# Down projection of a hybrid decoder block: which weight loads go to x1's old memory, and where one activation split stands

## The chip, the core and the metric

The kernel runs on one core of a Trainium2 chip. TensorE (PE) multiplies matrices, and PEld is its loading of weights; VectorE (DVE) and ScalarE (ACT) do elementwise work; GpSimd (POOL) does a little of it and issues some DMAs; SyncE (SP) issues most DMAs, in order. The metric is the time of one execution on the device, in microseconds (us).

## The reference, cut to what matters

One decoder block over 256 tokens of width 1024, all in float32: two token mixers (a gated linear recurrence and block attention), a gated merge, an output projection, a layer norm, a SwiGLU feed-forward network (FFN) of inner width 2816, and a second layer norm. The end is what matters here:

```python
x = layer_norm(DN_ALPHA * x + mixed, ln1_w, ln1_b)
h = jnp.einsum('bsd,df->bsf', x, w_ffn_in)
h_gate, h_up = jnp.split(h, 2, axis=-1)
y = jnp.einsum('bsf,fd->bsd', jax.nn.silu(h_gate) * h_up, w_ffn_down)   # the down projection
return layer_norm(DN_ALPHA * x + y, ln2_w, ln2_b)
```

## The kernel before

**Weights.** All weights come as 77 tiles of 128 x 2048 floats (1 MB), numbered 0 to 76 in the order of use. `stage` loads a tile into a buffer `raw` (SP), ScalarE rounds it to the high part `wh`, VectorE subtracts to get the low part `wl`, and TensorE makes three products of the high and low parts of weights and activations. The last reader of a raw buffer is VectorE's subtraction. The pools: `wraw` has three raw buffers, `whi` and `wlo` four each, taken in turn; `big` has 12 slots of the same size for everything else, and a slot is free when its last reader has run.

```python
wraw = pool("wraw", 3)
whi = pool("whi", 4)
wlo = pool("wlo", 4)
big = pool("big", 12)
```

**The down projection.** The FFN's inner width is worked in 11 blocks of two times 128 columns (`ffn_step`, with `q` the block's number), and block q's activations meet tile 66 and up of `w_ffn_down` in the order of `SEQUENCE`. `DOWN = "STTSTTSTPPP"` gives the kinds: the first eight tiles (66 to 73, blocks 2 to 9) are done with seven products instead of eight (`fast`), from a tile's four quarters and from sums of quarters; the last three (74 to 76, blocks 0, 1 and 10) are plain. A fast tile goes through `stage_fast` twice, as "corners" (three of its quarters, products `p1`, `p2`, `p3`) and as "sums" (four sums of quarters). For a tile of kind S (66, 69, 72) all four quarters are loaded with the corners and VectorE makes the sums in `cst` and a tile `sums` (lines 247 to 250). For a tile of kind T (67, 68, 70, 71, 73) DMAs made the sums in DRAM long before, and `rawsums` loads them.

**Where a raw load of a fast tile goes.** The sums of T tiles 68, 70, 71 and 73 go to a slot of `big`; the first T tile's sums (67) and all corners go to `wraw`. In `big` four slots come free about then: one half of x1's transposed parts `x1p` (the other half goes to `wb2`, the second norm's weights, loaded by GpSimd), `room` (the FFN's working memory), and the activations `as1`, `as2` of tiles that are done.

**The order.** In the last two FFN blocks and in the down projection TensorE, VectorE and ScalarE run in the order of the code (`manual_schedule`); SP's and GpSimd's order comes from a scheduler's own timeline. `fetch` runs ahead of TensorE by `LOOKAHEAD` = 3 tiles. The last block's `ffn_step` (block 10, plain) ends with `split(act_plain[q]...)`: ScalarE's cast `ap <- room` (line 191) and VectorE's subtraction (line 192).

**The end.** After tile 73's products `into_residual` (lines 1055 to 1064, VectorE) brings sums into `x1`; the plain tiles' products follow, the last ones in `edge` and `more`; VectorE, ScalarE and GpSimd make the second norm's statistics (lines 1104 to 1165) and SP stores four pieces.

Of the kernel before, what the change touches and what calls it, by code (L numbers as in the profile page):

```python
# [24 lines left out]
NF = FF // P  # L25
# [20 lines left out]
FAST = tuple(range(2, 2 + len(DOWN) - DOWN.count("P")))  # L46
PLAIN = tuple(q for q in range(NF // 2) if q not in FAST)
SEQUENCE = [PLAIN[DOWN[:i].count("P")] if s == "P" else FAST[i - DOWN[:i].count("P")] for i, s in enumerate(DOWN)]
SUMMED = [q for q, s in zip(SEQUENCE, DOWN) if s == "T"]
# [78 lines left out]
def hybrid_layer_kernel(ctx: ExitStack, tc, x, xw, vecs, bias, wts, ln1_w, ln1_b, ln2_w, ln2_b, consts, out):  # L128
# [12 lines left out]
    def slot(name, dt=F32):  # L141
        return big.tile([P, 2048], dt, tag="s8", name=name)

    def r32(ap):
        return ap.bitcast(F32)
# [32 lines left out]
    down = {t[1] // 2: i for i, t in enumerate(tiles) if t[0] == "w_ffn_down"}  # L178
# [6 lines left out]
    corners = {}  # L185
# [4 lines left out]
    def split(dst_h, dst_l, src):  # L190
        nc.scalar.copy(dst_h, src)
        nc.vector.tensor_sub(dst_l, src, r32(dst_h))
# [34 lines left out]
    quarters = lambda z: z.rearrange("p (b c) -> p b c", b=4)  # L227
# [13 lines left out]
    def stage_fast(i, kind):  # L241


        def make_sums(b):
            y, z = corners[i] = [v.rearrange("p (b c) -> p b c", b=2) for v in (
                cst, cp.tile([P, D], F32, tag="mv1", name=f"sums{i}"))]
            nc.vector.tensor_add(y, b[:, 1:3, :], b[:, 0:1, :].to_broadcast([P, 2, 512]))
            yield
            nc.vector.tensor_add(z[:, 0, :], b[:, 2, :], y[:, 0, :])
            nc.vector.tensor_add(z[:, 1, :], b[:, 3, :], z[:, 0, :])  # L250

        first = i == down[SUMMED[0]]
        raw = lambda: quarters(slot(f"raw{kind}{i}") if kind == "sums" and not first else
                               wraw.tile([P, 2048], F32, tag="raw", name=f"raw{kind}{i}"))
        h = quarters(whi.tile([P, 2048], F32R, tag="h", name=f"wh{kind}{i}"))
        l = quarters(wlo.tile([P, 2048], F32R, tag="l", name=f"wl{kind}{i}"))
        if kind == "corners":
            b = raw()
            n = 1 if i in summed else 0
            nc.sync.dma_start(b[:, n:4, :], quarters(wts[i])[:, n:4, :])  # L260
            sums = make_sums(b) if n == 0 else iter(())
            next(sums, None)
            h, l = h[:, 0:3, :], l[:, 0:3, :]
            nc.scalar.copy(h, b[:, 1:4, :])  # L264
            yield
            list(sums)
            nc.vector.tensor_sub(l, b[:, 1:4, :], r32(h))  # L267
            yield
        elif i in summed:
            z = raw()  # L270
            nc.sync.dma_start(z, quarters(summed[i]))
            nc.scalar.copy(h, z)  # L272
            yield
            nc.vector.tensor_sub(l, z, r32(h))  # L274
            yield
        else:
            for z, bs in zip(corners.pop(i), (slice(0, 2), slice(2, 4))):
                nc.scalar.copy(h[:, bs, :], z)
                yield
                nc.vector.tensor_sub(l[:, bs, :], z, r32(h[:, bs, :]))  # L280
                yield
        ready.append((h, l))

    def fetch(ahead=LOOKAHEAD):
        while state["next"] < len(loads) and len(ready) < 1 + ahead:
            list(stage())
        return ready.pop(0)
# [43 lines left out]
    def wide_pair(name, a, p, tag, twos=0):  # L331


        wh, wl = fetch()
        pss = []
        for f in range(2):
            ps = p.tile([P, 2, T], F32, tag=tag, name=f"{name}{f}")
            wcol = slice(f * P, (f + 1) * P)
            n = twos if f == 0 else 0
            for ks in [(k, k + 1) for k in range(0, 2 * n, 2)] + [(k,) for k in range(2 * n, KC)]:  # L340
                for k in ks:
                    nc.tensor.matmul(ps, wh[:, k, wcol], a.both(k), start=(k == 0), stop=False)  # L342
                for k in ks:
                    nc.tensor.matmul(ps[:, 0, :], wl[:, k, wcol], a[0, k, slice(0, T)],  # L344
                                     start=False, stop=(k == KC - 1))
            pss.append(ps)
        return pss
# [69 lines left out]
    with tc.manual_schedule(engines={ET.PE, ET.DVE, ET.Activation}):  # L417

        first = [slot(f"xw{k}")[:, 0:T + D] for k in range(KC)]
# [423 lines left out]
    def bcast(name, w, b):  # L843
        t = slot(name).rearrange("p (a d) -> p a d", a=2)
        nc.gpsimd.dma_start(t[:, 0, :], w[0].partition_broadcast(P))
        nc.gpsimd.dma_start(t[:, 1, :], b[0].partition_broadcast(P))
        return t
# [48 lines left out]
    act_plain = {q: apl[i // 2][:, i % 2] for i, q in enumerate(PLAIN)}  # L896

    def fast_parts(i):
        if i == 0:
            tiles = [klp.tile([P, H * P], F32R, tag="kl", name="ash"), cp.tile([P, D], F32R, tag="bgr", name="asl")]  # L900
        elif i == len(FAST) - 1:
            tiles = [apl[-1][:, 1].rearrange("p u k t -> p (u k t)"), cp.tile([P, 7 * P], F32R, tag="masks", name="asl7")]
        else:
            both = slot(f"as{i}", F32R)
            tiles = [both[:, 0:1024], both[:, 1024:2048]]
        return [z[:, 0:7 * P].rearrange("p (b t) -> p b t", b=7) for z in tiles]
# [94 lines left out]
    def ffn_step(j):  # L1001
        q = j // 2
        z = room[:, q % 2]
        gate, up = [z[:, b:b + 4, :].rearrange("p (f t) c -> p f (t c)", f=2) for b in (0, 4)]
        for nm, p, tag, s in [("g", mm, "mm", gate), ("u", aux, "aux", up)]:
            for f, ps in enumerate(wide_pair(f"f{nm}{j}", x1p, p, tag)):
                nc.scalar.copy(s[:, f, :], ps[:, 1, :])
                nc.vector.tensor_add(s[:, f, :], ps[:, 0, :], s[:, f, :])
            if nm == "g":
                nc.scalar.activation(s, s, AF.Silu)  # L1010
        nc.vector.tensor_mul(gate, gate, up)
        if q in PLAIN:
            split(act_plain[q][:, 0], act_plain[q][:, 1], gate)
            return

        nc.vector.tensor_sub(z[:, 4, :], z[:, 0, :], z[:, 2, :])
        nc.vector.tensor_sub(z[:, 5, :], z[:, 4, :], z[:, 1, :])
        nc.vector.tensor_sub(z[:, 6, :], z[:, 1, :], z[:, 0, :])
        nc.vector.tensor_add(z[:, 7, :], z[:, 3, :], z[:, 5, :])
        act_fast[q] = fast_parts(FAST.index(q))  # L1020
        split(*act_fast[q], z[:, 1:8, :])

    for j in range(EARLY, NF - 2 * ORDERED, 2):
        ffn_step(j)

    with tc.manual_schedule(engines={ET.PE, ET.DVE, ET.Activation}):
        for j in range(NF - 2 * ORDERED, NF, 2):
            ffn_step(j)
        wb2 = bcast("wb2", ln2_w, ln2_b)
        bank = lambda p, n: p.tile([P, 512], F32, tag="aux" if p is aux else "mm", name=n)  # L1030
        p2, p4, p1, p5 = [bank(mm, f"wp{i}") for i in (2, 4, 1, 5)]
# [9 lines left out]
        def fast(q):  # L1041
            ah, al = act_fast[q]
            for products in [((p1, 0, 0), (p2, 2, 2), (p3, 6, 1)),
                             ((p4, 1, 3), (p5, 3, 0), (p6, 4, 2), (p7, 5, 1))]:
                wh, wl = fetch()
                for ps, a, b in products:
                    stop = q == FAST[-1] and (ps in shared or ps is p2)
                    nc.tensor.matmul(ps, ah[:, a, :], wh[:, b, :], start=(q == begins[id(ps)]), stop=False)
                    nc.tensor.matmul(ps, ah[:, a, :], wl[:, b, :], start=False, stop=False)
                    nc.tensor.matmul(ps, al[:, a, :], wh[:, b, :], start=False, stop=stop)  # L1050
# [17 lines left out]
        for i, q in enumerate(SEQUENCE):  # L1068
            if q in FAST:
                fast(q)  # L1070
                if q == FAST[-1]:
                    into_residual()
                continue
            tile_q = [(2 * q,) + fetch()]
            if i < len(SEQUENCE) - HOLD_DOWN:
                for part in late:
                    rows_pass([part], lhs, 1, tile_q, first=2 * begins[id(part[0])], **ends)
            else:
                held += tile_q
            for part in early:  # L1080
                rows_pass([part], lhs, 0, tile_q, first=2 * begins[id(part[0])], **ends)
# [9 lines left out]
        sums = sm.tile([P, 2 * HOLD_DOWN], F32, tag="bst", name="wsum")  # L1091
# [113 lines left out]
```

## Time and profile before

| | |
|---|---|
| median of 3 runs | 488.55 us (488.53 to 488.66) |
| the profiled execution | 488.99 us, span 487.2 us |
| granted TensorE clock, mean | 0.998 |
| TensorE (PE), busy | 477.8 us, 98% |
| VectorE (DVE), busy | 387.9 us, 80% |
| ScalarE (ACT), busy | 293.8 us, 60% |
| GpSimd (POOL), busy | 57.6 us, 12% |
| DMA, all queues | 108.70 MB, mean 223 GB/s |

The profile has one page and views that are asked of the trace: windows (busy time of each engine in a stretch), timelines (start, duration, engine, line, operation, tiles; in brackets the engine's idle time before it and what ended it), the chain of waits followed back from the end, and the DMA view (issues, with the time until the data has landed). Times are us from the span's start. A matmul's shown duration overlaps the next one's: the distance of starts is what counts. `wp` is any of the products' PSUM banks.

### The profile page before, as it was taken

How to read it: one execution, taken by the hardware profiler on the slowest of the kernel's cores; microseconds unless marked ns; L12 is line 12 of the kernel's file. 1: busy time of each engine (PE TensorE's matmuls, PEld its weight loads, DVE VectorE, ACT ScalarE, POOL GpSimd, SP SyncE). 2: the span in 40 equal slices, each digit the busy share in tenths (PEclk: the TensorE clock that was granted, in tenths of full speed). 3: DMA queues.
4: the chain of work that ended last, by engine and by line, in shares of the span. 5: the costliest groups of instructions: out<-in, count | busy, mean ns of one | idle time of the engine just before them, and what ended most of it. 6: DMA issues, size and time to landing. Idle time of an engine off the chain costs nothing.

```text
span 487.2 us, 7433 instructions
## 1 busy us (share of the span) xinstructions
PE 477.8 (98%) x2956; PEld 408.8 (84%) x2956; DVE 387.9 (80%) x503; ACT 293.8 (60%) x407; POOL 57.6 (12%) x62
## 2 busy tenths in 40 slices
PE   8999999999999999999999999999999999999994
PEld 8888888788899888888888888888888888877884
DVE  4979895799947889998567778754887779689995
ACT  6698666447565787765743353455565564566762
POOL 0000000000024522422002001012110000000120
PEclk9999999999999999999999999999999999999999
DMA  8977438522853354468979853599999654299642
GB/s 307 414 308 262 174 120 297 214 105 88 295 200 112 118 206 166 160 219 279 264 270 283 227 221 139 187 295 291 301 243 300 204 199 154 92 414 381 220 111 87
DMA packets 21667, 108.70 MB, mean 223 GB/s; under 512 B 2432, under 2 KB 4224, under 8 KB 11904
## 3 DMA queue, kind: packets, MB, share of 16 engines
q1 hardware_dynamic: 16128, 98.13, 54.7%
q0 software_dynamic: 5360, 9.96, 10.4%
q8 instruction: 23, 0.38, 0.3%
q10 hardware_dynamic: 144, 0.13, 0.1%
q14 instruction: 12, 0.10, 0.1%
HBM read 105.59 MB, written 11.53 MB: 240 GB/s over the span
## 4 chain that ended last, share of the span: by engine, by line
PE 86%; DVE 6%; DMA 3%; issue 2%; ACT 1%; DVEq 0%; POOLq 0%; POOL 0%; SPq 0%; ACTq 0%
PE fu L342 7%; PE fg L342 7%; PE fg L344 3%; PE fu L344 3%; PE hq L342 3%; PE mq L342 2%; PE mk L342 2%; DMA rawsums<-sums 2%; PE mv L393 2%; PE gb L393 2%; PE hg L393 2%; PE hf L367 2%; PE hq L344 2%; PE mv L395 2%; PE ga L393 2%
## 5 line engine op out<-in xcount | busy, mean ns | idle before, releaser
L223 DVE TENSOR_TENSOR wl<-raw,wh 128x2048 fp32r<-128x2048 f32 (+1 forms) x70 | 160.4, 2296 | 55.4 <-ACT wh L221 55.1
L221 ACT CAST wh<-raw 128x2048 fp32r<-128x2048 f32 (+1 forms) x70 | 131.6, 1887 | 58.8 <-PE fg L342 14.0
L342 PE MATMUL fg<-x1p,wh 128*128 128x512 f32 x144 | 50.5, 394 | 0.0
L342 PE MATMUL fu<-x1p,wh 128*128 128x512 f32 x144 | 50.4, 394 | 0.0
L344 PE MATMUL fg<-x1p,wl 128*128 128x256 f32 x144 | 40.0, 278 | 0.0
L344 PE MATMUL fu<-x1p,wl 128*128 128x256 f32 x144 | 39.9, 277 | 0.0
L342 PEld LDWEIGHTS fu<-x1p,wh 128*128 128x128 f32 x144 | 27.0, 187 | 6.2
L342 PEld LDWEIGHTS fg<-x1p,wh 128*128 128x128 f32 x144 | 27.0, 187 | 6.1
L344 PEld LDWEIGHTS fg<-x1p,wl 128*128 128x128 f32 x144 | 27.1, 188 | 0.1
L344 PEld LDWEIGHTS fu<-x1p,wl 128*128 128x128 f32 x144 | 27.1, 188 | 0.0
L745 POOL TENSOR_TENSOR rtk<-rtk,cst 128x512 f32<-128x512 f32 x4 | 6.2, 1560 | 163.7 <-ACT rtk L743 163.7
L342 PE MATMUL hq<-xp,wh 128*128 128x512 f32 x64 | 22.2, 394 | 0.0
L344 PE MATMUL hq<-xp,wl 128*128 128x256 f32 x64 | 17.7, 277 | 0.0
L342 PE MATMUL mq<-xp,wh 128*128 128x512 f32 x48 | 17.0, 398 | 0.0
L342 PE MATMUL mk<-xp,wh 128*128 128x512 f32 x48 | 16.7, 395 | 0.0
L235 POOL DMA_DIRECT2D sums<-sums x10 | 8.1, 810 | 66.9 <-DMA sums<-in_wts_dram 33.6
L267 DVE TENSOR_TENSOR wlcorners<-rawcorners,whcorners 128x1536 fp32r<-128x1536 f32 x8 | 14.0, 1752 | 2.1 <-ACT whcorners L264 2.1
L342 PEld LDWEIGHTS hq<-xp,wh 128*128 128x128 f32 x64 | 12.0, 188 | 2.8
L235 POOL DMA_DIRECT2D sums<-in_wts_dram x10 | 8.4, 988 | 41.1 <-DMA sums<-in_wts_dram 41.1
L274 DVE TENSOR_TENSOR wlsums<-rawsums,whsums 128x2048 fp32r<-128x2048 f32 x5 | 11.4, 2287 | 2.2 <-ACT whsums L272 2.2
L344 PE MATMUL mq<-xp,wl 128*128 128x256 f32 x48 | 13.2, 281 | 0.0
L264 ACT CAST whcorners<-rawcorners 128x1536 fp32r<-128x1536 f32 x8 | 11.8, 1476 | 1.7 <-DMA rawcorners<-in_wts_dram 1.7
(371 smaller groups left out, 1339.7 us busy)
## 6 DMA issues: line engine op xcount, KB each, us to landing
raw<-in_wts_dram SPq DMA_DIRECT2D x68, 1024.0 KB, 4.9
sums<-in_wts_dram SPq DMA_DIRECT2D x10, 512.0 KB, 8.8
rawsums<-sums SPq DMA_DIRECT2D x5, 1024.0 KB, 9.1
xw<-in_xw_dram SPq DMA_DIRECT2D x6, 640.0 KB, 9.4
rawcorners<-in_wts_dram SPq DMA_DIRECT2D x5, 768.0 KB, 6.0
rawcorners<-in_wts_dram SPq DMA_DIRECT2D x3, 1024.0 KB, 8.1
sums<-in_wts_dram POOLq DMA_DIRECT2D x10, 256.0 KB, 9.1
sums<-sums POOLq DMA_DIRECT2D x10, 256.0 KB, 6.5
```

The costliest lines, as they stand in the source:

```text
L221: nc.scalar.copy(h[:, ks, :], raw[:, ks, :])
L223: eng.tensor_sub(l[:, ks, :], raw[:, ks, :], r32(h[:, ks, :]))
L235: more = lambda dst, src: nc.gpsimd.dma_start(dst, src, accum_op=ALU.add)
L264: nc.scalar.copy(h, b[:, 1:4, :])
L267: nc.vector.tensor_sub(l, b[:, 1:4, :], r32(h))
L274: nc.vector.tensor_sub(l, z, r32(h))
L342: nc.tensor.matmul(ps, wh[:, k, wcol], a.both(k), start=(k == 0), stop=False)
L344: nc.tensor.matmul(ps[:, 0, :], wl[:, k, wcol], a[0, k, slice(0, T)], start=False, stop=(k == KC - 1))
L367: nc.tensor.matmul(ps, wh[:, kk, wcol], xp.both(k), start=False, stop=False)
L393: nc.tensor.matmul(pss[t], ah[:, kk, ts], wh[:, k, :], start=(kk == 0), stop=False)
L395: nc.tensor.matmul(pss[t], ah[:, kk, ts], wl[:, k, :], start=False, stop=(kk == KC - 1))
L745: nc.gpsimd.tensor_mul(tmp, tmp, bc(sin))
```

## The change

Two things. In `stage_fast` the raw loads that go to `big` are now the corners, from the fourth fast tile on (69 to 73); all sums of T tiles, and the corners of 66, 67 and 68, go to `wraw`. In the last block the split of its activations is left to a later place: `ffn_step` returns `gate`, and the split is written behind `fast(FAST[0])`, the products of tile 66. In code that is after the fetches that `fast` made.

```diff
-        first = i == down[SUMMED[0]]
-        raw = lambda: quarters(slot(f"raw{kind}{i}") if kind == "sums" and not first else
+        beside = kind == "corners" and i not in [down[q] for q in SEQUENCE[0:3]]
+        raw = lambda: quarters(slot(f"raw{kind}{i}") if beside else
                                wraw.tile([P, 2048], F32, tag="raw", name=f"raw{kind}{i}"))
...
         if q in PLAIN:
-            split(act_plain[q][:, 0], act_plain[q][:, 1], gate)
-            return
+            if q < NF // 2 - 1:
+                split(act_plain[q][:, 0], act_plain[q][:, 1], gate)
+            return gate
...
-            ffn_step(j)
+            last_gate = ffn_step(j)
...
                 fast(q)
+                if q == FAST[0]:
+                    split(act_plain[PLAIN[-1]][:, 0], act_plain[PLAIN[-1]][:, 1], last_gate)
                 if q == FAST[-1]:
```

SP's loads from tile 68's corners on, before (the first number in a name is the tile's; the last is a buffer's):

```order
L260 DMA rawcorners68_3984<-in_wts_dram 128x1536
L271 DMA rawsums68_4002<-sums4_85 128x2048
L260 DMA rawcorners69_4017<-in_wts_dram 128x2048
L271 DMA rawsums70_4072<-sums6_86 128x2048
L260 DMA rawcorners70_4054<-in_wts_dram 128x1536
L260 DMA rawcorners71_4087<-in_wts_dram 128x1536
L271 DMA rawsums71_4105<-sums7_87 128x2048
L271 DMA rawsums73_4175<-sums9_88 128x2048
L260 DMA rawcorners72_4120<-in_wts_dram 128x2048
L260 DMA rawcorners73_4157<-in_wts_dram 128x1536
```

The same place on SP now:

```order
L260 DMA rawcorners68_3982<-in_wts_dram 128x1536
L260 DMA rawcorners69_4017<-in_wts_dram 128x2048
L271 DMA rawsums68_4002<-sums4_85 128x2048
L271 DMA rawsums70_4072<-sums6_86 128x2048
L271 DMA rawsums71_4105<-sums7_87 128x2048
L260 DMA rawcorners70_4054<-in_wts_dram 128x1536
L260 DMA rawcorners71_4087<-in_wts_dram 128x1536
L271 DMA rawsums73_4175<-sums9_88 128x2048
L260 DMA rawcorners72_4120<-in_wts_dram 128x2048
L260 DMA rawcorners73_4157<-in_wts_dram 128x1536
```

The corners of 69 moved ahead of the sums of 68, and the sums of 71 ahead of the corners of 70 and 71; raw74 to raw76 follow in both. What frees the memory of each now: 69 x1p's half (TensorE's last `fu` product), 70 `room` (the split of the last block's activations), 71 and 72 `as1` and `as2` (TensorE's products of tiles 67 and 68), 73 the corners of 69; the sums of 68 the corners of 67, those of 70 the sums of 67, those of 71 the corners of 68, those of 73 the sums of 68 (VectorE's subtractions).

ScalarE where the last block ends and the down projection begins, the difference:

```order
 L1007 COPY room_3056<-fu201_3932 128x256
+L272 CAST whsums67_3965<-rawsums67_3967 128x2048
+L264 CAST whcorners68_3980<-rawcorners68_3982 128x1536
 L191 CAST ap1_2624<-room_3056 128x512
-L272 CAST whsums67_3967<-rawsums67_3969 128x2048
-L264 CAST whcorners68_3982<-rawcorners68_3984 128x1536
 L272 CAST whsums68_4000<-rawsums68_4002 128x2048
 L264 CAST whcorners69_4015<-rawcorners69_4017 128x1536
```

The cast of the last block's activations moved behind two casts of weights, and nothing else moved here. VectorE's subtractions moved in the same way; TensorE's order is the same.

## The prediction

> In what follows c68 is the load of tile 68's corners (`rawcorners68`), s68 that of its sums (`rawsums68`), wlc68 and wls68 the VectorE subtractions that end their splits, and raw76 the last plain load.
>
> **What bounds the kernel now.** First the page's head.
>
> ```profile
> span 487.2 us, 7433 instructions
> PE 477.8 (98%) x2956; PEld 408.8 (84%) x2956; DVE 387.9 (80%) x503; ACT 293.8 (60%) x407; POOL 57.6 (12%) x62
> ```
>
> TensorE is busy for 98% of the span. The change touches the down projection alone, so I next read the windows there: length, busy time of PE, PEld, DVE, ACT and POOL with counts, granted clock, DMA share, GB/s.
>
> ```profile
> 430.00:440.00 10.00, 8.61 (x36) 6.47 (x36) 8.81 (x8) 6.61 (x5) 0.00 (x0) 1.00 1.02 424
> 440.00:450.00 10.00, 10.00 (x45) 7.97 (x44) 10.00 (x7) 6.86 (x5) 0.00 (x0) 1.00 0.95 366
> 450.00:460.00 10.00, 10.00 (x46) 8.22 (x45) 9.93 (x9) 8.15 (x6) 0.72 (x1) 1.00 0.56 199
> ```
>
> TensorE's only loss is in 430 to 440, where the DMA engines are full (share 1.02, 424 GB/s). From 440 to 460 VectorE is as full as TensorE: whatever delays VectorE before 440 is not made up. TensorE's timeline (start, duration) shows the stalls:
>
> ```profile
> 429.45 0.39 PE L1050 MATMUL wp<-whcorners,as 128*128 128x512 f32 x1
> 429.68 0.39 PE L1048 MATMUL wp<-whsums,as 128*128 128x512 f32 x1
> 430.19 0.50 PE L1049 MATMUL wp<-wlsums,as 128*128 128x512 f32 x1
> 430.53 0.39 PE L1050 MATMUL wp<-whsums,as 128*128 128x512 f32 x1
> ...
> 434.86 0.39 PE L1048 MATMUL wp<-whsums,as 128*128 128x512 f32 x1
> 435.27 0.50 PE L1049 MATMUL wp<-wlsums,as 128*128 128x512 f32 x1
> 435.61 0.40 PE L1050 MATMUL wp<-whsums,as 128*128 128x512 f32 x1
> ...
> 437.90 0.39 PE L1048 MATMUL wp<-whcorners,as 128*128 128x512 f32 x1
> 439.53 0.50 PE L1049 MATMUL wp<-wlcorners,as 128*128 128x512 f32 x1 [1.25 <-DVE wlcorners L267]
> 439.87 0.39 PE L1050 MATMUL wp<-whcorners,as 128*128 128x512 f32 x1
> ```
>
> Starts are 0.23 apart (429.45 to 429.68), so two steps take 0.46. The sums of tile 67 lose 0.85 - 0.46 = 0.39 us, those of 68 lose 0.29, the corners of 69 lose 1.51. The chain of waits (start, length, what) says behind what these lie:
>
> ```profile
> 423.04 7.84 DMA rawsums<-sums
> ...
> 430.98 1.92 ACT whsums L272
> ...
> 432.93 2.29 DVE wlsums L274
> 435.22 1.15 DVE cst L247
> ...
> 457.71 5.25 DMA raw<-in_wts_dram
> ...
> 465.01 2.29 DVE wl L223
> ```
>
> s68 lands at 430.88, ScalarE splits it, and from 432.93 on VectorE runs without a pause; at 457.71 raw76 is issued, and its VectorE work at 465.01 leads into the second layer norm. So two loads set this stage: s68 at its head, raw76 at its end. The change moves both.
>
> **Part 1: the split of `last_gate`.** It goes behind the casts of s67 and c68, on ScalarE and VectorE. ScalarE's rows, then VectorE's:
>
> ```profile
> 425.38 0.62 ACT L191 CAST ap<-room 128x512 fp32r<-128x512 f32 x1 [1.96 <-DVE room L1011]
> 425.91 1.91 ACT L272 CAST whsums<-rawsums 128x2048 fp32r<-128x2048 f32 x1
> ...
> 433.46 1.48 ACT L264 CAST whcorners<-rawcorners 128x1536 fp32r<-128x1536 f32 x1 [0.56 <-DMA rawcorners<-in_wts_dram]
> ...
> 438.79 1.48 ACT L264 CAST whcorners<-rawcorners 128x1536 fp32r<-128x1536 f32 x1
> ...
> 456.26 1.91 ACT L221 CAST wh<-raw 128x2048 fp32r<-128x2048 f32 x1
> ...
> 480.61 0.47 ACT L1110 ACTIVATE z<-more,n2sum 128x256 f32<-128x256 f32 x1 [0.39 <-PE more L861]
> ```
>
> ```profile
> 426.03 0.69 DVE L192 TENSOR_TENSOR ap<-room,ap 128x512 fp32r<-128x512 f32 x1 [0.69 <-ACT ap L191]
> ...
> 443.33 2.29 DVE L274 TENSOR_TENSOR wlsums<-rawsums,whsums 128x2048 fp32r<-128x2048 f32 x1
> ...
> 455.93 1.75 DVE L267 TENSOR_TENSOR wlcorners<-rawcorners,whcorners 128x1536 fp32r<-128x1536 f32 x1
> 457.60 2.28 DVE L274 TENSOR_TENSOR wlsums<-rawsums,whsums 128x2048 fp32r<-128x2048 f32 x1
> ...
> 467.22 0.68 DVE L1055 SCALAR_TENSOR_TENSOR x<-x,wp 128x512 f32<-128x512 f32 x1
> ...
> 478.46 0.22 DVE L1155 TENSOR_SCALAR n2sum<-wp,n2sum 128x1 f32<-128x1 f32 x1 [0.25 <-PE wp L861]
> ```
>
> ScalarE waited 1.96 us for VectorE and worked 0.53 before it came to s67. That goes: s67's cast starts 425.91 - 1.96 - 0.53 = 423.4, 2.5 earlier, and wls67 is 2.5 earlier too. Tile 67's stall of 0.39 goes. The moved split costs 0.62 and 0.69 on two engines that now wait for s68 until past 433: nothing. Its readers are tile 10's products, 30 us later: nothing.
>
> **Part 2: c69 ahead of s68.** On SP c69 takes s68's place and slot (x1's second half, free when the last `fu` product has read it), and s68 takes c69's (free after wlc67). Their rows on SP, and the DMA view of their two issues, with the time from issue to landing; last, s67, issued at 405 into an idle queue:
>
> ```profile
> 423.04 0.33 SPq L271 DMA_DIRECT2D rawsums<-sums  x1
> 423.98 0.33 SPq L260 DMA_DIRECT2D rawcorners<-in_wts_dram  x1
> ```
>
> ```profile
> rawsums<-sums SPq DMA_DIRECT2D x1, 1024.0 KB, 7.8
> ```
>
> ```profile
> rawcorners<-in_wts_dram SPq DMA_DIRECT2D x1, 1024.0 KB, 9.4
> ```
>
> ```profile
> rawsums<-sums SPq DMA_DIRECT2D x1, 1024.0 KB, 4.7
> ```
>
> The second landed at 423.98 + 9.4 = 433.4, 2.5 after the first; 1.05 MB at 424 GB/s are 2.47 us. So the two stood in line, and each took its share of a full queue. Both have the same size, and both issue times stay, so I take c69 to land at 430.88 and s68 at 433.36: **+2.48 us**. The lower bound is 0 (s68 lands as now, whatever is ahead of it), or even 4.7 after its issue, at 428.7; the upper is 2.48 and a little more. I take the end that the two landings show.
>
> Behind s68 on ScalarE and VectorE, in order, stand c69's cast, its sums and all later splits, although c69 is there already. wls68 starts at 433.36 + 0.10 + 1.92 + 0.03 = 435.41, not 432.93. TensorE, 0.39 ahead, comes to it at 434.7 and now stalls some 3.1 us, where it stalled 0.29. The 1.51 for the corners of 69 stay, since they are four VectorE instructions behind wls68. The rest is VectorE's unbroken row: all of it, and TensorE, +2.48.
>
> The Trainium skill ("DMA: Bandwidth & Descriptors", section "Queues, rings and completion order") says that each DMA engine takes descriptors in ring order, but that a later transfer may complete before an earlier one, so that completion is not first in, first out for an issuing engine. By that s68 could land no later than now, and the sum would be the second rival's below; the trace bears it out little, since the two landings kept their order by one whole transfer.
>
> **Part 3: the loads after these.** s71 goes ahead of c70 and c71. With s70 at 435.85 (one transfer behind s68), s71 lands near 438.3, c70, 0.75 MB, near 440.2; its cast stood at 438.79 and is now due at 441.27. It fits by 1.1 us. That is what is late next. raw74 waits for wls70 now: 443.33 + 2.29 + 2.48 = 448.1, some 10 us before its cast (456.26 + 2.48): nothing. c72 and c73 are ahead of their casts in the same way.
>
> **Part 4: raw76.** The pool `wraw` has three buffers, taken in turn. Before, the three loads ahead of raw76 in it were c73, raw74 and raw75, so it waited for the reader of c73, wlc73 (455.93 + 1.75 = 457.68). Now they are s73, raw74 and raw75, so it waits for wls73, the next VectorE instruction: 457.60 + 2.28 = 459.88. That is **+2.2 us** on top of the 2.48. Nothing covers it: the chain above goes through this load. With 5.0 to 5.25 us to landing (the chain's 5.25) raw76's subtraction comes 4.4 to 4.7 late, at 469.5 rather than 465.01.
>
> TensorE hardly minds. It took the product that needs it here:
>
> ```profile
> 469.27 0.39 PE L860 MATMUL wp<-wl,ap 128*128 128x512 f32 x1
> ```
>
> at 469.27 + 2.48 = 471.75, and the subtraction ends at 471.8 to 472.0: 0.0 to 0.3. But the residual (467.22 on) and the second norm stand behind it on VectorE in one row. Before the end this row has two rests, 0.25 us for TensorE's `edge` (478.46) and 0.39 on ScalarE for `more` (480.61), and these take up 0.64.
>
> **Sum.** 2.48 + 2.2 = 4.7 at raw76's wait, less up to 0.25 for a shorter landing, less 0.64: +3.8 to +4.1; I take +4.0. The profiled execution took 488.99 (span 487.2), 0.44 above the median of the runs, 488.55. It becomes 493.0, and the median 492.5.
>
> **Rivals.**
> - *TensorE sets the end, raw76's lateness is absorbed.* If the norm's VectorE row has more rest than the two I count, what is left is TensorE's shift: 2.48 + 0.0 to 0.3 = +2.7, 491.2. For it: TensorE's last product is waited for today. Against it: from 467.22 to 478.46 TensorE makes this VectorE row rest for 0.25 only.
> - *s68 lands as now.* Then part 2 costs nothing, c70 (440.2 against 438.79, mostly covered by VectorE's backlog) some 0.3, raw76 2.2, less 0.64: about +1.7, 490.2. Against it: the 2.48 between the two landings. The Trainium skill's rule above points here.
> - *Not slower: the queue holds nothing back.* If the 7.84 us of s68 were its own and not the line's, and it now came after 4.7 us like s67, it would land at 428.7; wls68 would start 2.2 earlier, which cancels raw76's 2.2, and the three stalls go: -0.6 to 0, 488.2. It decides from a landing of s68 before 429.5. Against it: a share of 1.02.
> - *Worse: c70 or c71 come late too.* If the line moves 1.1 us slower than I have it, each further us lands on VectorE: 493.6.
>
> **How the numbers follow.** The forecast has 0.70, then 0.10, 0.06, 0.07 and 0.07 for the rivals in order. The range runs from the second rival's 490.2 to 493.8, just above the last: 0.93 of the cases, less the forecast's own tails. This kernel's runs cannot tell less than 0.2%, 0.98 us, from no change; only the third rival is within or beyond it on the fast side: faster 0.03, same 0.04, slower 0.93.
>
> **What would show it.** In the trace after: TensorE's stall before the sums of 67 gone; c69 landed near 430.9 and s68 near 433.4, with ScalarE waiting for s68 about 6 us; a TensorE stall of some 3 us before wls68's products; VectorE without a pause from 435.4 to 464; raw76 issued near 462.4, and VectorE or ScalarE, not TensorE, released last. A landing of s68 at 431 or earlier, or an end released by `more`, would make me wrong.

## The result, and the profile after

The changed kernel takes 492.21 us (median of 6 runs, 491.9 to 494.12) against 488.54 us (488.33 to 488.82) of the kernel before beside it: a ratio of 1.0079, 95% interval [1.0063, 1.0095]: slower by 0.8%, clear of the noise. The profiled execution took 492.29 us, its span 490.5 us at a granted clock of 0.997.

The chain of waits after, at the same places as before (start, length, what):

```profile
423.85 9.26 DMA rawsums<-sums
...
433.20 1.92 ACT whsums L272
...
435.14 2.29 DVE wlsums L274
437.44 1.14 DVE cst L247
...
459.82 2.29 DVE wlsums L274
...
462.13 4.78 DMA raw<-in_wts_dram
...
468.96 2.29 DVE wl L223
471.25 0.59 DVE x L1056
```

s68 landed at 423.85 + 9.26 = 433.1 and not at 430.88, wls68 began at 435.14 and not at 432.93, and raw76 was issued at 462.13 instead of 457.71, right behind wls73 instead of wlc73. The same windows as before (length; PE, PEld, DVE, ACT and POOL busy; clock; DMA share; GB/s):

```profile
430.00:440.00 10.00, 7.48 (x32) 5.65 (x31) 4.79 (x5) 4.33 (x3) 0.00 (x0) 1.00 1.01 424
440.00:450.00 10.00, 8.77 (x38) 6.67 (x37) 10.00 (x8) 8.63 (x6) 0.00 (x0) 1.00 0.86 344
450.00:460.00 10.00, 10.00 (x45) 8.26 (x45) 9.93 (x9) 7.11 (x6) 0.00 (x0) 1.00 0.51 184
```

VectorE is busy for 4.79 us of the ten from 430 on, where it had 8.81, with the DMA engines as full as before (424 GB/s in both). The rows of ScalarE, VectorE and TensorE there, with idle time and its end in brackets:

```profile
423.18 1.92 ACT L272 CAST whsums<-rawsums 128x2048 fp32r<-128x2048 f32 x1
...
426.38 0.62 ACT L191 CAST ap<-room 128x512 fp32r<-128x512 f32 x1
433.20 1.91 ACT L272 CAST whsums<-rawsums 128x2048 fp32r<-128x2048 f32 x1 [6.20 <-DMA rawsums<-sums]
...
441.01 1.47 ACT L264 CAST whcorners<-rawcorners 128x1536 fp32r<-128x1536 f32 x1
```

```profile
425.14 2.29 DVE L274 TENSOR_TENSOR wlsums<-rawsums,whsums 128x2048 fp32r<-128x2048 f32 x1
...
435.14 2.29 DVE L274 TENSOR_TENSOR wlsums<-rawsums,whsums 128x2048 fp32r<-128x2048 f32 x1 [5.45 <-ACT whsums L272]
...
443.88 1.75 DVE L267 TENSOR_TENSOR wlcorners<-rawcorners,whcorners 128x1536 fp32r<-128x1536 f32 x1
```

```profile
429.32 0.39 PE L1051 MATMUL wp<-whcorners,as 128*128 128x512 f32 x1
429.54 0.39 PE L1049 MATMUL wp<-whsums,as 128*128 128x512 f32 x1
429.77 0.39 PE L1050 MATMUL wp<-wlsums,as 128*128 128x512 f32 x1
...
434.08 0.39 PE L1051 MATMUL wp<-whcorners,as 128*128 128x512 f32 x1
435.17 0.51 PE L1049 MATMUL wp<-whsums,as 128*128 128x512 f32 x1 [0.70 <-ACT whsums L272]
437.49 0.51 PE L1050 MATMUL wp<-wlsums,as 128*128 128x512 f32 x1 [1.82 <-DVE wlsums L274]
...
441.75 0.50 PE L1050 MATMUL wp<-wlcorners,as 128*128 128x512 f32 x1 [1.23 <-DVE wlcorners L267]
```

The cast of s67 runs at 423.18 instead of 425.91 and TensorE passes to the sums of 67 without a pause. What that wins, ScalarE and VectorE then spend waiting for s68.

### The profile page after: what moved, and what is told of

It is laid out like the page before. It is cut to its first block, busy times and chain, and to the rows that moved or that the text cites. A ratio compares the mean times of both kernels' runs of the same rounds, so it can differ in the third digit from the quotient of the medians.

```text
span 490.5 us, 7432 instructions
## 1 busy us (share of the span) xinstructions
PE 478.2 (97%) x2956; PEld 409.4 (83%) x2956; DVE 387.7 (79%) x503; ACT 293.5 (60%) x407; POOL 57.6 (12%) x62
## 4 chain that ended last, share of the span: by engine, by line
PE 82%; DVE 9%; DMA 3%; issue 2%; ACT 2%; DVEq 0%; POOLq 0%; POOL 0%; ACTq 0%
PE fg L342 6%; PE fu L342 5%; PE fg L344 3%; PE hq L342 3%; PE fu L344 3%; PE mq L342 2%; PE mk L342 2%; DMA rawsums<-sums 2%; DVE wlcorners L267 2%; PE mv L393 2%; PE gb L393 2%; PE hg L393 2%; PE hf L367 2%; PE hq L344 2%; PE ga L393 1%
## 5 line engine op out<-in xcount | busy, mean ns | idle before, releaser
L272 ACT CAST whsums<-rawsums 128x2048 fp32r<-128x2048 f32 x5 | 9.6, 1912 | 7.4 <-DMA rawsums<-sums 6.2
```

## The experiments

Theory: the split costs and brings nothing; s68 behind c69 in the line costs some 2.2 us, and raw76's wait for wls73 as much again, less a little slack at the end. The rivals: the moved split has a part in the loss; the lateness of raw76 is absorbed; s68's landing alone doesn't matter. Each run stands beside the kernel before on the same chip, which had a median of 488.9 us with the first four runs, 488.63 with the next four and 488.74 with the last two.

### 1. The split alone

The changed kernel, its raw loads in the places of before:

```diff
-        beside = kind == "corners" and i not in [down[q] for q in SEQUENCE[0:3]]
-        raw = lambda: quarters(slot(f"raw{kind}{i}") if beside else
+        first = i == down[SUMMED[0]]
+        raw = lambda: quarters(slot(f"raw{kind}{i}") if kind == "sums" and not first else
```

> Only the split of the last block's activations is moved; the raw loads keep their old places. Theory (the time lies in two loads, sums of 68 and raw76): 488.5, within 0.2% of before; tile 67's TensorE stall goes, and the one for the sums of 68 grows by the same 0.4 us. Rival (the split, now between casts of weights, costs): 490 or more. Rival (the split's move is worth its stall): 488.1.

488.57 us (11 runs), ratio 0.9993 [0.9984, 1.0001]: the same as before. VectorE's rows of wls67 and wls68:

```profile
424.56 2.29 DVE L274 TENSOR_TENSOR wlsums<-rawsums,whsums 128x2048 fp32r<-128x2048 f32 x1
...
432.02 2.29 DVE L274 TENSOR_TENSOR wlsums<-rawsums,whsums 128x2048 fp32r<-128x2048 f32 x1 [2.90 <-ACT whsums L272]
```

wls67 comes early, and VectorE then waits 2.90 us for s68's split where it waited 1.12. The later split also frees `room` later, so s70, which still goes there, is issued at 429.19 (426.79 before), behind c70 and c71, and lands at 440.46; ScalarE waits 1.21 us for it and VectorE not at all. An engine that is freed in front of a late load waits for it longer.

### 2. The places alone

The changed kernel with the split of `last_gate` back in `ffn_step`.

> Only the raw loads change place; the split stays where it was. Theory: all of the loss, 492.2 (+3.7 over before), the sums of 68 landing near 433.2 and raw76 issued near 462.2. Rival (half of the loss is the split's): 490.4.

492.37 us, ratio 1.0075 [1.0062, 1.0088]. s68 landed at 433.28 and raw76 was issued at 462.30. The places carry the whole loss. `room` is free earlier here, so c70 went ahead of s70 and s71 (it landed at 435.39), and the loss is the same: in the changed kernel c70's place behind them cost nothing.

### 3. raw76 early again

In the changed kernel, tile 73's sums go to `big` and its corners to `wraw`, so that raw76 waits for wlc73.

```diff
-        beside = kind == "corners" and i not in [down[q] for q in SEQUENCE[0:3]]
+        swap = i == down[FAST[-1]]
+        beside = (kind == "sums" if swap else kind == "corners") and i not in [down[q] for q in SEQUENCE[0:3]]
```

> The changed kernel, but tile 73 puts its sums beside and its corners in the raw pool, so that raw76 waits for the corners' subtraction as before. Theory: raw76 is issued near 459.9 and not 462.1, TensorE's last products release the end again, and only the 2.2 to 2.5 us of the sums of 68 are left: 490.8 to 491.0. Rival (raw76's lateness is absorbed in the norm's slack): no change, 492.2.

490.98 us, ratio 1.0048 [1.0034, 1.0061]. raw76 was issued at 459.74 and landed at 464.91. So raw76's wait for one more VectorE instruction is worth 492.37 - 490.98 = 1.4 us of the 3.5 between before and the second experiment, though its issue came 2.56 earlier. By the ratios, the changed kernel's 1.0079 against 1.0048, it is 1.5. Of the rest 0.46 is a longer landing (5.17 us against 4.71), and most is slack at the end: VectorE waits 0.28 us for TensorE's `edge` again, and ScalarE 0.39 for `more`.

### 4. s68 early again

In the changed kernel, SP issues s68 ahead of c69 as before; the places stay.

```diff
-            nc.sync.dma_start(b[:, n:4, :], quarters(wts[i])[:, n:4, :])
+            load = nc.sync.dma_start(b[:, n:4, :], quarters(wts[i])[:, n:4, :])
+            if i == down[SEQUENCE[3]]:
+                tc.keep_in_program_order(load)
...
-            nc.sync.dma_start(z, quarters(summed[i]))
+            load = nc.sync.dma_start(z, quarters(summed[i]))
+            if i == down[SEQUENCE[2]]:
+                tc.keep_in_program_order(load)
```

> The changed kernel, but on SP the sums of 68 are issued ahead of the corners of 69, both into the same memory as in the changed kernel. Theory: the sums of 68 land near 430.7 again (first in the line), TensorE's 2.5 us stall before their low part goes, and only raw76's 2.2 less the slack at the end is left: 489.9 to 490.2. Rival (the sums of 68 are late because of the buffer they wait for, or what else the change moved in the queue): 491.5 to 492.2.

491.45 us, ratio 1.0058 [1.0045, 1.007]: a miss, just below the rival's range. Yet s68 was early, as the chain's row for it shows (424.30 + 6.87 = 431.17). ScalarE's next casts, and VectorE's subtraction behind the second of them, show what came in its place (lines 264 and 267 are 266 and 269 in this kernel):

```profile
424.30 6.87 DMA rawsums<-sums
```

```profile
438.13 1.05 ACT L282 CAST whsums<-sums 128x1024 fp32r<-128x1024 f32 x1 [0.32 <-DVE sums L250]
442.00 1.48 ACT L266 CAST whcorners<-rawcorners 128x1536 fp32r<-128x1536 f32 x1 [2.82 <-PE wp L1055]
```

```profile
443.51 1.76 DVE L269 TENSOR_TENSOR wlcorners<-rawcorners,whcorners 128x1536 fp32r<-128x1536 f32 x1 [1.48 <-ACT whcorners L266]
```

ScalarE stood 2.82 us idle before the cast of c70, and VectorE 1.48 us before wlc70. The trace puts ScalarE's wait on a product of TensorE that ended at 441.97, but c70 itself, issued at 430.23, landed at 441.90, 0.07 us before that. Experiment 5 tells which of the two it was. Two things made c70 so late. It stood behind s70 and s71; and it came 3.26 us behind s71 (438.64), where 0.75 MB at 424 GB/s take 1.85: 15 of the 16 DMA engines had brought their share by 440.51, and the last one at 441.90, 1.39 us after them. Had it come with them, VectorE would have waited some 0.1 us and not 1.48 (an estimate from these rows).

### 5. and 6. All loads in the order of the tiles

Experiment 5: in the changed kernel every load of a fast tile is kept in the order of the code on SP, so that c70 comes ahead of s70 and s71. Experiment 6: the same with the edit of experiment 3.

```diff
-            nc.sync.dma_start(b[:, n:4, :], quarters(wts[i])[:, n:4, :])
+            tc.keep_in_program_order(nc.sync.dma_start(b[:, n:4, :], quarters(wts[i])[:, n:4, :]))
...
-            nc.sync.dma_start(z, quarters(summed[i]))
+            tc.keep_in_program_order(nc.sync.dma_start(z, quarters(summed[i])))
```

> The changed kernel, with all loads of fast tiles issued on SP in the order of the tiles (s68, c69, c70, s70, c71, s71, c72, c73, s73). Theory (with s68 early, it was c70, put behind s70 and s71, that held the earlier experiment at 491.45; with c70 ahead of them nothing before 455 us is late, and only raw76, which still waits for wls73, is): c70 lands by 436.5 and its cast waits for no load; raw76 issued about 459.9; the time is that of before plus the 2.2 us of raw76 less 0.4 to 0.64 us of slack: 489.9 to 490.5. Rival (the loss comes from the places themselves or from the total of the loads, and another one is late in c70's stead, by as much): 491.2 to 492.2. Rival (raw76's lateness costs nothing by itself): 488.3 to 488.9.

> The same order of loads, and tile 73's sums in a place in big and its corners in wraw, so that raw76 waits for wlc73 as it did before. Theory (s68's landing, c70's behind it, and raw76's issue are all that the new places cost): raw76 issued 457.2 to 457.8, and nothing is lost: 488.2 to 488.7, as before. Rival (something else in the new places or in the moved split costs): 489.5 or more.

Experiment 5 took 489.88 us, ratio 1.0028 [1.0016, 1.0039], at the low edge of what was expected. c70 landed at 435.23 and its cast no longer waits:

```profile
437.09 1.05 ACT L278 CAST whsums<-sums 128x1024 fp32r<-128x1024 f32 x1 [0.33 <-DVE sums L250]
438.05 1.47 ACT L264 CAST whcorners<-rawcorners 128x1536 fp32r<-128x1536 f32 x1
```

TensorE's wait for the corners of 69 ended at 438.78 here (at 439.82 in experiment 4), and the cast went ahead of these products by 0.7 us. So it needs nothing from them, and it was the load that held it in experiment 4: c70's late landing is worth 491.45 - 489.88 = 1.6 us. That is the price of its place behind s71 and of the one late share together. In experiment 5 a share was late too, but of c71 (fifteen by 439.55, the last at 441.30), and VectorE did not wait for it. From wls68's start to raw76's issue it is 432.18 to 459.16, 26.98 us, where before it was 432.93 to 457.71, 24.78: the 2.20 of one VectorE subtraction, and beside experiment 6 they cost 489.88 - 488.72 = 1.2 us of time.

Experiment 6 took 488.72 us, ratio 1.0001 [0.9992, 1.001], with raw76 issued at 457.43. With s68, c70 and raw76 back in time nothing of the loss is left, although the loads still go to the new places and the split to its new one.

### 7. to 10. What else stands in the line ahead of s68

If s68 sets this stage, bringing it in earlier than before should win something. The two loads of `wb2` (0.5 MB each, on GpSimd's queue) are issued at 422.08 and 422.65, just ahead of s68, land at 426.90 and 429.85, and nobody needs them before the second layer norm (the times in the first expectation below are those of experiment 4's trace). Experiment 7 is the kernel before, with the loads in the order of the tiles as in experiment 5, and `wb2` behind the products of a later tile; experiment 8 adds the changed kernel's moved split; experiment 9 has `wb2` late, the new places, the split moved, the loads in order and tile 73 as in experiment 3; experiment 10 is experiment 8 with `wb2` where it was.

```diff
-        wb2 = bcast("wb2", ln2_w, ln2_b)
...
                 fast(q)
+                if q == SEQUENCE[6]:
+                    wb2 = bcast("wb2", ln2_w, ln2_b)
```

> The kernel before, with the loads in the order of the tiles and the two broadcast loads of wb2 (POOL, 0.5 MB each, issued at 422.4 and 423.0, landing 427.2 and 428.6) moved behind wls68, where nothing waits for them. Theory (the loads share one line of about 424 GB/s: what is queued ahead of s68 sets when it lands, and s68 sets wls68): without the 1 MB ahead of it s68 lands about 2.4 us earlier than before's 430.88, wls68 begins earlier by 1.0 to 2.0 us until TensorE or ScalarE holds it, and the time falls by 1.0 to 1.6 us: 487.1 to 487.7. Rival (the POOL queue's loads do not hold up SP's): s68 lands as in before, 488.3 to 488.8. Rival (the 1 MB now holds up c71 or s71 and gives the gain back): s68 early, and 488.3 to 489.2.

> The same as the last, and last_gate's split behind the first tile's products, as in the changed kernel. Theory (with s68 early, VectorE is no longer idle behind the first tile, so TensorE sets the pace there and the 0.39 us stall before tile 67's products now counts): 0.3 to 0.5 us below the last run, 486.6 to 487.3. Rival (VectorE sets the pace, as in both kernels, and where the split stands is of no account): within 0.2 us of the last run. Rival (the split now delays wlc68 or wls68, VectorE having no idle time left): 0.3 to 1.9 us above it.

> The changed kernel's places and moved split, loads in the order of the tiles, tile 73's sums in big (raw76 waits for wlc73), and wb2's two loads behind wls68. Theory (which loads go to wraw is of no account in itself; only when s68, c70 and raw76 land is): s68 lands before 427.5, TensorE runs without a stall from 422 to 460 as in the run with the places of before, and the time is the same as there: 486.0 to 486.6. Rival (the new places keep a cost of their own once nothing else is late): 486.8 or more.

> The kernel before, with the loads in the order of the tiles and the moved split, and wb2's loads where they were, ahead of s68. Theory (wb2's 1 MB shares the line with s68 and puts it 2 us or more later than the 426.27 of the run without it): s68 lands between 428.4 and 430.5, VectorE waits for it again before wls68, and the time is 487.0 to 488.7. Rival (the order of the loads and the split made the gain, not the 1 MB): 486.0 to 486.6.

| | split | `wb2` | places | s68 issued, landed | us | ratio to before |
|---|---|---|---|---|---|---|
| 7 | as before | late | as before | 421.83, 426.67 | 488.21 | 0.9992 [0.9984, 1.0001] |
| 8 | moved | late | as before | 421.46, 426.27 | 486.24 | 0.9951 [0.9938, 0.9963] |
| 9 | moved | late | new | 423.66, 428.61 | 486.28 | 0.9953 [0.994, 0.9967] |
| 10 | moved | early | as before | 422.82, 430.51 | 488.60 | 0.9999 [0.999, 1.0008] |

Experiment 7 missed: the early s68 is there, and no gain that is clear of the noise; 488.21 lies between the theory's range and the second rival's. Its rows of VectorE and ScalarE:

```profile
428.02 2.29 DVE L274 TENSOR_TENSOR wlsums<-rawsums,whsums 128x2048 fp32r<-128x2048 f32 x1 [1.12 <-ACT whsums L272]
430.23 1.75 DVE L267 TENSOR_TENSOR wlcorners<-rawcorners,whcorners 128x1536 fp32r<-128x1536 f32 x1
431.90 2.29 DVE L274 TENSOR_TENSOR wlsums<-rawsums,whsums 128x2048 fp32r<-128x2048 f32 x1
...
447.24 2.29 DVE L274 TENSOR_TENSOR wlsums<-rawsums,whsums 128x2048 fp32r<-128x2048 f32 x1 [0.99 <-ACT whsums L272]
```

```profile
445.29 1.91 ACT L272 CAST whsums<-rawsums 128x2048 fp32r<-128x2048 f32 x1 [2.29 <-DMA rawsums<-sums]
```

s68 was there at 426.67 (its place, x1's half, was free sooner than the one it had, so it was also issued 1.2 us earlier), but wls67 came as late as before (428.02), since the split stood ahead of it, so wls68 gained only 1.0 us; and that went at 447.24, where VectorE waited for s71. Two things made s71 late. The moved `wb2`, though issued 2 us after it on GpSimd's queue, shared the line with it: fifteen shares of s71 were there at 443.64, 6.22 us behind s70, where c71's and its own 1.84 MB take 4.33 at 424 GB/s. This is the second rival. And its sixteenth share came at 445.19, 1.55 us after the others; without that, VectorE would not have waited here (an estimate: the cast would have ended near 445.7, and VectorE was free at 446.25). The profiled execution was the slowest of the eleven, 489.04, and the fastest, 487.43, is in the theory's range. So what `wb2` takes back by itself stays open.

With the split moved as well (experiment 8) TensorE has no stall at all:

```profile
430.00:440.00 10.00, 10.00 (x46) 8.28 (x45) 9.93 (x8) 7.41 (x6) 1.14 (x2) 1.00 1.00 398
440.00:450.00 10.00, 10.00 (x46) 8.29 (x45) 9.78 (x8) 6.07 (x5) 0.00 (x0) 1.00 1.01 410
```

It beats both kernels, and experiment 7 by 2.0 us where 0.3 to 0.5 was expected. The moved split, worth nothing alone (experiments 1 and 10), is worth 2.0 us here: the reason given for it, TensorE's 0.39, was too small, because it brings forward the whole row of VectorE, wls68 to 429.63 from 431.90 (0.4 of this the run had won ahead of the stage), and VectorE's wait for s71 falls from 0.99 to 0.2.

Experiment 9 shows that the places have no price of their own: the time is the same. There s68 landed 2.3 us later than in experiment 8, since its place waits for wlc67; that misses the landing expected (before 427.5), and VectorE waits 1.14 us for it. Experiment 10 takes the gain away by putting `wb2` back in front. Its s68 is issued 1.4 us later than in experiment 8, and takes 7.7 us to land instead of 4.8. The later issue is not the cause: in experiment 9 s68 was issued later still (423.66) and landed in 4.95. So it is the 1 MB ahead. VectorE waits 2.95 us again:

```profile
432.55 2.29 DVE L274 TENSOR_TENSOR wlsums<-rawsums,whsums 128x2048 fp32r<-128x2048 f32 x1 [2.95 <-ACT whsums L272]
```

## Why the prediction was right, point by point

- **Part 1, the split costs and brings nothing: right.** TensorE's stall for the sums of 67 went, experiment 1 gave 0.9993 [0.9984, 1.0001], and the time turned up in the wait for s68, as said. That it depends on s68 being late was left open; experiments 8 and 10 showed it.
- **Part 2, s68 one transfer later: right.** Forecast 430.88 and 433.36 for the two landings, measured 422.91 + 7.7 = 430.6 and 433.1. The two stalls of TensorE before wls68's product came to 437.49 - 434.08 - 0.46 = 2.95 us, forecast 3.1, and the 1.5 for the corners of 69 stayed. With raw76 put right (experiment 3) this part alone costs 490.98 - 488.9 = 2.1 us.
- **Part 3, the later loads: right, with more in hand than forecast.** c70 landed at 439.95, its cast began at 441.01: 1.06 us in hand, forecast 1.1. VectorE came to wlc70 only at 443.88, where the cast had ended at 442.48; so c70 could have come some 2.4 us later before VectorE waited.
- **Part 4, raw76: right.** Issued at 462.13 (forecast 462.4), its subtraction 3.95 us late. The forecast had 4.4 to 4.7; of the 0.75 to its upper end 0.47 is raw76's landing in 4.78 us instead of 5.25, the rest its issue. The slack at the end is as counted: from 3.95 late at wl76, VectorE reached the last output (line 1116) at 485.35, 3.33 late, so 0.62 were absorbed, against 0.64 forecast. VectorE's row for `edge`, which waited 0.25 for TensorE before, now waits for nothing, and nor does ScalarE's for `more`, which waited 0.39. The chain's last piece is VectorE's, as it was before:

```profile
482.07 0.21 DVE L1158 TENSOR_SCALAR n2sum<-wp,n2sum 128x1 f32<-128x1 f32 x1
...
485.35 1.41 DVE L1116 SCALAR_TENSOR_TENSOR y<-y,n2sum,wb 128x512 f32<-128x512 f32 x2 [0.27 <-POOL n2sum L1169]
```

```profile
483.72 0.46 ACT L1113 ACTIVATE z<-more,n2sum 128x256 f32<-128x256 f32 x1
```

- **The sum.** +3.67 us between the medians and +3.3 in the profiled executions, against +4.0: the term that was too large is raw76's landing, by 0.2 to 0.5, and its issue came 0.3 earlier than forecast.
- **The rivals.** The first, raw76's lateness is absorbed, is out by experiment 3: taking the lateness away brings 1.4 us, near the 2.2 less 0.64 of the sum. The third is out by the landing of s68 at 433.1 and not before 429.5, the fourth by VectorE, which was busy for all of 440 to 450; its bound of 1.1 us was ScalarE's alone, and VectorE's was 2.4. The second, s68 lands as now, was priced at 490.2, though its terms, 0.3 + 2.2 - 0.64, make 1.86 and not 1.7. Experiment 4 is that case, and took 491.45. The step that failed there is c70's "some 0.3": it assumed c70 whole at 440.2, and fifteen shares were there at 440.51, but the last at 441.90, in a run whose VectorE was ahead by what s68 had won. As for order, SP's loads landed in the order of their issue in this stretch in all twelve profiles. The Trainium skill's "DMA: Bandwidth & Descriptors", section "Queues, rings and completion order", says that completion is not first in, first out for an issuing engine; its example is a later transfer on one DMA engine beside an earlier one on sixteen. Both c69 and s68 landed in sixteen shares, so that example is not this case, and the prediction took more from it for s68 than it gives. On one queue no run here shows a later load landing first, and the forecast was right not to count on it. Between queues one does: in experiment 8 GpSimd's load of `wb2`, issued at 432.37, landed at 441.67, ahead of s71, issued by SP at 429.70, at 442.10.

## What to carry to other kernels

When the DMA engines are full, price a load by the bytes that stand ahead of it, on all queues, and look for bytes there that nobody needs yet. On another queue even bytes issued after it can take their share of the line, as `wb2` did from s71 in experiment 7. A new buffer assignment moves loads in two ways, by the place that each takes in the queue and by the reader that it has to wait for; both are read from the order of issue before anything is run. An edit that brings nothing alone can be worth several times its stall once the wait that covers it is gone, so try the two together.

## What the runs showed that was not expected

One DMA engine of the sixteen fell about 1.4 us behind the other fifteen near 440 us, and stayed behind for the loads after: in experiment 4 the shares of c70 had landed by 440.5 on fifteen engines and at 441.9 on the last, those of c71 by 442.4 and at 443.8. A load counts as landed with its slowest share. In the changed kernel the same lag met c71 (441.8 and 443.3) and not c70. At that time the trace has one packet on an instruction queue (window of 438 to 440 us in experiment 4):

```profile
q1 hardware_dynamic: 148, 0.81, 97.4%
q8 instruction: 1, 0.02, 3.4%
```

One packet of 0.02 MB, 3.4% of 16 engines over 2 us, is 1.1 us of one engine. That this fetch of instructions makes the lag is an inference from the time and the size, and no run was made to test it. But the packet moved with the kernels: it starts between 435.7 us (experiment 8) and 441.2 (the changed kernel), once in this stretch of each of the twelve profiles. From 421 us to the packet, no load of SP had its last share more than 0.43 us behind the fifteenth. In eleven of the profiles the first or second of SP's loads to land after the packet had it 0.47 to 1.98 us behind. The twelfth, experiment 6, has the packet at 438.9, and the next six loads have no share more than 0.12 us late. So the packet is the likely cause, and not the shown one: the profile does not tell which DMA engine carried it, and in one run it cost nothing.
